# Sampled memory attention in eight units instead of twelve, the spread of token factors one place later

## The chip, the cores and the metric

The kernel runs on one core of one Trainium2 chip. The metric is the device time of one execution in microseconds (us); the median of three runs of the kernel before is 2639.46 us (2638.61 to 2641.45). The engines are TensorE (PE), VectorE (DVE), ScalarE (ACT) and GpSimd (POOL); SyncE (SP) issues most of the DMAs.

## The reference, cut to what matters

One inference step of a two-layer decoder trunk, for a prompt of 1024 tokens and for 8 samples of 8 tokens that share all weights. In every layer a mixing block is followed by cross-attention into a memory and by a convolutional feed-forward block. The change lies in the cross-attention, for the samples' part above all: each of the 8 samples has its own cached keys and values of 256 memory tokens, 4 heads of 128.

```python
def mem_attend(h, k, v, w_q, q_gain, w_o):
    q = rmsnorm((h @ w_q).reshape(N, T, MEM_HEADS, MEM_HD), q_gain)
    s = jnp.einsum('nthd,nmhd->nhtm', q, k) * (MEM_HD ** -0.5)
    pr = jax.nn.softmax(s, axis=-1)
    o = jnp.einsum('nhtm,nmhd->nthd', pr, v)
    return o.reshape(N, T, MEM_WIDTH) @ w_o
...
    xp = xp + mem_attend(rmsnorm(xp, ln_mem[l]), mk, mv, m_w_q[l], m_q_gain[l], m_w_o[l])
    xs = xs + mem_attend(rmsnorm(xs, ln_mem[l]), cache_mem_k[l], cache_mem_v[l], m_w_q[l],
                         m_q_gain[l], m_w_o[l])
    fp, cp = conv_ffn(rmsnorm(xp, ln_ffn[l]), zc, f_w_up[l], ...)
```

## The kernel before

The 1088 tokens lie in nine tiles of 128 (the last, tile 8, has the 64 sample tokens) and in three chunks of 384, 384 and 320 columns. `mem(l, rs)` does the cross-attention of one layer and runs twice, once per layer; `ffn(l)` follows each time.

`mem` first loops over the nine tiles: `qproj` (the query projection, matmuls at L259 to L261), `scores` of the tile before (L830), its softmax on DVE and ACT, and `trp` of the tile before that, which transposes the probabilities (L167 from `k`, copies at L846 and L847). Then comes the out-projection: for each chunk c two halves of four blocks m, and for each (c, m) one product of twelve matmuls (L259 to L261) that writes a `psa` buffer. `x_out` adds the old x to it (DVE L323, L325), squares it (ACT L303) and adds the square to the chunk's sum `acc` (L305, on DVE for odd m, on POOL for even m), and stores the new x by SP in `xq` (L330).

The samples' attention is cut into pieces by the generator `all_samples()`, and the program calls `next(parts)` between the products. Two sets a and b hold four samples each. Their pieces are:
- `keys(j)`: load sample j's keys (512 KB, SP, one of three stage buffers `st`), 16 transposes in two groups (L167 from `st`) into two PSUM buffers, copied by DVE (L884) and ACT (L882) to a `k` tile
- `score`: 32 matmuls (L890); `softmax` (L810 to L822, and four loads of values by SP)
- `trans`: two transposes and a copy (L906); `values`: 16 matmuls (L912), then DVE L915 and L918; `finish`: one transpose and a copy (L924)

Behind the products of a chunk stand `norm_chunk(c)`, which sums `acc` over the partitions (PE L352, then DVE L335 and three powers on POOL, L336), and `factors(c)`, that is `spread`: three diagonals on DVE (L387), three matmuls that spread them over the partitions (PE L388) and a copy into `rvq` (DVE L391). `build()` multiplies x by `rvq` (DVE L1094, `hx`) and makes the operands of `ffn`'s first products from it (L1105, L1106, L1111); their weights come by L1061 and are split at L1069 and L1070.

The order of PE is the order in which the program is written; the other engines' orders are set by a scheduler at build time. `psA()` and `psB()` hand out PSUM buffers `psa` and `psb`, four of each. Loads and stores go through SP's queue in order.

Before, the samples' pieces stand so. `a.keys(0)` follows tile 7 in the loop and `a.keys(1)` stands ahead of the out-projection; both use `psa`. With chunk 0's products m = 3, 4, 5 come `a.keys(2)`, `a.keys(3)`, the score of a; with chunk 1's products m = 1, 4, 5, 6 the trans of a, its values, `b.keys(0)`, `b.keys(1)`; with m = 7 the finish of a and `b.keys(2)`. At j == 4, between chunk 1 and chunk 2, stand `b.keys(3)`, the score of b, `norm_chunk(1)`, `factors(1)`, `build()` and the rest of b. `norm_chunk(0)` and `factors(0)` follow chunk 1's product m = 2.

Of the kernel before, what the change touches and what calls it, by code (L numbers as in the profile page):

```python
# [71 lines left out]
def kernel(  # L72
# [22 lines left out]
    def f(ap):  # L95
        return ap.bitcast(F32)
# [4 lines left out]
    def psB():  # L101
        return pb.tile([128, 512], F32, tag="b", name="psb")
# [48 lines left out]
    def small(tag="s", w=8, bufs=12):  # L151
        return sm.tile([128, w], F32, tag=tag, name=tag, bufs=bufs)
# [117 lines left out]
    def tile_of(t):  # L270
        return t // 3, (t % 3) * 128, (128 if t < 8 else 64)
# [76 lines left out]
    def norm_chunk(c):  # L348
        ps = psB()
        for t in range(3 * c, 3 * c + 3):  # L350
            _, o, w = tile_of(t)
            mm(ps[:w, 2 * (t % 3):2 * (t % 3) + 2], lhsT=acc[c][:, o:o + w], rhs=ones[:, 0:2], start=True, stop=True)  # L352
        for t in range(3 * c, 3 * c + 3):
            w = tile_of(t)[2]
            xr[t] = small(f"r{t}", 1, 1)
            rsq(xr[t][:w], ps[:w, 2 * (t % 3):2 * (t % 3) + 1], 1.0 / D)
# [384 lines left out]
    def mem(l, rs):  # L741
# [4 lines left out]
        def factors(c, pl=tmp):  # L746
            o, n = CHS[c]
            spread(c, xr, pl, rvq[:, o:o + n])

        with ExitStack() as es:  # L750
# [17 lines left out]
            def build():  # L768

                tcp = es.enter_context(pool(f"mem{l}tc"))  # L770
                R["tc"] = 1
                for j in range(4):
                    up_operands(l, 0, j, xq, rvq, B0, tcp)
# [153 lines left out]
            def all_samples():  # L927
                a, b = Samples(0), Samples(1)
                for x, y in ((a, None), (b, a)):
                    x.keys(0, psB if y else psA)  # L930
                    yield
                    x.keys(1, psB if y else psA)
                    yield
                    if y:
                        y.finish()
                    x.keys(2)
                    yield
                    x.keys(3)
                    yield
                    x.score()  # L940
                    x.softmax()
                    for _ in range(4):
                        yield
                    x.trans()
                    for _ in range(3):
                        yield
                    x.values()
                    yield
                yield
                yield  # L950
                b.finish()

            for i in range(NT):
# [7 lines left out]
                if i == 6:  # L961
                    parts = all_samples()
# [4 lines left out]
            for j, (hf, c) in enumerate([(0, 0), (1, 0), (0, 1), (1, 1), (0, 2), (1, 2)]):  # L967
                o, n = CHS[c]
                if j == 4:
                    for _ in range(2):  # L970
                        next(parts)
                    norm_chunk(1)
                    factors(1)
                    build()
                    for _ in parts:
                        pass
                if hf == 0 and c:
                    sp = [split_act(s3p, n, otf[:, k, o:o + n]) for k in range(4)]
                    if c == 2:
                        old = []  # L980
                        for i in range(4):
                            rd = f(s3p.tile([128, 2, 384], F32R, tag="s3", name="rd"))[:, :, :n]
                            nc.sync.dma_start(out=rd, in_=xd[:, 2 * i:2 * i + 2, :])
                            old += [rd[:, 0], rd[:, 1]]
                for m in range(4 * hf, 4 * hf + 4):
                    ps = psA()
                    w = wo[m // 2]
                    mo = 128 * (m % 2)
                    for k in range(4):
                        mm3(ps[:, :n], w[:, 0, k, mo:mo + 128], w[:, 1, k, mo:mo + 128], sp[k][:, 0, :n], sp[k][:, 1, :n], k == 0, k == 3)  # L990
                    x_out(c, m, ps, xq, [old[m]] if c == 2 else [f(xh[c][:, m, :]), f(xl[c][:, m, :])], rvq[:, o:o + n] if c == 2 else None)
                    if c == 0 and m == 1:
                        trp(7)
                    elif c == 0 and m == 2:
                        trq(8)
                        expand_q()
                        pv(2)
                        es2.close()
                        rvp = rs.enter_context(tc.tile_pool(name=f"rv{l}", bufs=1, reuse_waits="tile", side="right"))
                        rvq = rvp.tile([128, 1088], F32, name="rvq")  # L1000
                        gtail = rvp.tile([128, 18, HB], F32, name="gtail")
                    elif c > 0 or m > 2:
                        next(parts, None)
                    if c == 1 and m == 2:
                        norm_chunk(0)
                        factors(0)
        return xq, rvq, gtail, B0, factors

# [805 lines left out]
```

## Time and profile before

| | |
|---|---|
| median of three runs | 2639.46 us (2638.61 to 2641.45) |
| the profiled execution | 2642.09 us |
| its span, first to last instruction | 2640.3 us |
| mean granted TensorE clock | 0.965 of full speed |
| PE busy | 2494.3 us, 94% of the span |
| DVE busy | 1971.8 us, 75% |
| ACT busy | 1235.5 us, 47% |
| POOL busy | 447.6 us, 17% |

The profile is that of one execution, and its own time stands beside its span: durations below come from it. A busy share is a mean over all stages. The first `mem` lies at some 337 to 556 us of the span, the second at some 1690 to 1900. Rows give a start in us, a duration in us, the engine, the line of the kernel and the tile, the number of instructions in the row (x8), and in brackets the idle time of the engine just ahead and what ended it. In rows of matmuls the ends overlap with the next start.

### The profile page before, as it was taken

Reading aid. Unit: us, or ns where it says so; the run is one execution under the profiler, and the core shown is the slowest. Engines: PE = TensorE matmul, PEld = TensorE weight load, DVE = VectorE, ACT = ScalarE, POOL = GpSimd, SP = SyncE. Lnnn points to the kernel's source line nnn. Section 1 sums busy time; section 2 is a strip of 40 time slices with the busy share of each in tenths; the row PEclk is TensorE's granted clock in tenths of the full one; section 3 lists DMA queues with packets and bytes.
Section 4 is the critical chain, followed back from the end, with each engine's and each line's share of the span. In section 5 each row is a group of like instructions: output and inputs, shape, how many; then the busy total and the mean of one; then the engine's idle time right before and its main releaser. Section 6 shows DMA issues by size and latency. Waiting matters only on the chain. (4 is left out here: it accounts for less than half of the span.)

```text
span 2640.3 us, 46213 instructions
## 1 busy us (share of the span) xinstructions
PE 2494.3 (94%) x17136; PEld 2311.1 (88%) x17136; DVE 1971.8 (75%) x4551; ACT 1235.5 (47%) x2705; POOL 447.6 (17%) x418
## 2 busy tenths in 40 slices
PE   8999999779999998999999989998699999989898
PEld 7998988679999998999876768887599999989898
DVE  7646965797878786788767777856987878776885
ACT  7324645355554544333555554552555554544231
POOL 2516532110000001110133333421100000011100
PEclk9999999889999999999999998999799999999999
DMA  8302213533334236654211021115333334256642
GB/s 276 117 12 71 64 37 104 169 96 121 125 99 133 95 126 216 209 192 140 67 39 48 1 65 58 59 41 179 105 106 127 121 111 133 92 182 249 218 144 83
DMA packets 229345, 305.53 MB, mean 116 GB/s; under 512 B 17793, under 2 KB 189919, under 8 KB 229118
## 3 DMA queue, kind: packets, MB, share of 16 engines
q1 hardware_dynamic: 215806, 236.82, 28.3%
q0 software_dynamic: 13312, 65.74, 6.8%
q8 instruction: 135, 2.21, 0.4%
q14 instruction: 92, 0.75, 0.1%
HBM read 217.79 MB, written 84.63 MB: 115 GB/s over the span
## 5 line engine op out<-in xcount | busy, mean ns | idle before, releaser
L1069 ACT ACTIVATE w<-st 128x512 fp32r<-128x512 f32 (+2 forms) x532 | 299.9, 572 | 396.9 <-PE psb L1023 116.2
L1070 DVE TENSOR_TENSOR w<-st,w 128x512 fp32r<-128x512 f32 (+2 forms) x532 | 325.9, 617 | 175.0 <-ACT w L1069 167.5
L1021 PE MATMUL psa<-b,w 128*128 128x272 f32 x1056 | 309.2, 293 | 41.2 <-ACT b L1105 12.2
L1022 PE MATMUL psa<-b,w 128*128 128x272 f32 x1056 | 307.1, 291 | 10.1 <-DVE b L1106 10.1
L1021 PE MATMUL psa<-big,w 128*128 128x272 f32 x1056 | 309.8, 293 | 3.7 <-ACT x L1379 1.7
L1023 PE MATMUL psa<-big,w 128*128 128x272 f32 x1056 | 309.3, 293 | 0.5 <-DVE w L1070 0.5
L1022 PE MATMUL psa<-big,w 128*128 128x272 f32 x1056 | 308.3, 292 | 0.0
L1023 PE MATMUL psa<-b,w 128*128 128x272 f32 x1056 | 307.7, 291 | 0.0
L1021 PEld LDWEIGHTS psa<-b,w 128*128 128x128 f32 x1056 | 201.0, 190 | 44.8 <-ACT b L1105 12.8
L1021 PE MATMUL psb<-b,w 128*128 128x272 f32 x792 | 230.6, 291 | 0.0
L1023 PE MATMUL psb<-b,w 128*128 128x272 f32 x792 | 230.3, 291 | 0.0
L1023 PE MATMUL psb<-big,w 128*128 128x272 f32 x792 | 229.4, 290 | 0.5 <-DVE w L1070 0.5
L1021 PE MATMUL psb<-big,w 128*128 128x272 f32 x792 | 229.0, 289 | 0.0
L1022 PE MATMUL psb<-b,w 128*128 128x272 f32 x792 | 229.0, 289 | 0.0
L1022 PE MATMUL psb<-big,w 128*128 128x272 f32 x792 | 228.3, 288 | 0.0
L260 PE MATMUL psa<-s,w 128*128 128x384 f32 (+1 forms) x576 | 198.6, 345 | 15.3 <-DVE s L361 15.0
L1022 PEld LDWEIGHTS psa<-b,w 128*128 128x128 f32 x1056 | 201.2, 191 | 12.5 <-DVE b L1106 12.5
L1021 PEld LDWEIGHTS psa<-big,w 128*128 128x128 f32 x1056 | 202.5, 192 | 6.1 <-ACT x L1379 2.2
L1023 PEld LDWEIGHTS psa<-big,w 128*128 128x128 f32 x1056 | 203.5, 193 | 0.7 <-DVE w L1070 0.7
L1022 PEld LDWEIGHTS psa<-big,w 128*128 128x128 f32 x1056 | 202.8, 192 | 0.0
L259 PE MATMUL psa<-s,w 128*128 128x384 f32 (+1 forms) x576 | 199.0, 345 | 3.1 <-ACT s L360 3.1
L1023 PEld LDWEIGHTS psa<-b,w 128*128 128x128 f32 x1056 | 201.1, 190 | 0.0
(365 smaller groups left out, 6584.2 us busy)
## 6 DMA issues: line engine op xcount, KB each, us to landing
st<-in_f_w_up_dram SPq DMA_DIRECT2D x88, 512.0 KB
hd<-big SPq DMA_DIRECT2D x264, 136.0 KB
hd<-m SPq DMA_DIRECT2D x176, 136.0 KB
big<-hd POOLq DMA_DIRECT2D x48, 408.0 KB, 6.5
st<-in_f_w_down_dram SPq DMA_DIRECT2D x48, 384.0 KB
b<-hd POOLq DMA_DIRECT2D x18, 816.0 KB, 7.0
big<-hd POOLq DMA_DIRECT2D x18, 816.0 KB, 7.1
ks<-in_m_w_kv_dram SPq DMA_DIRECT2D x16, 512.0 KB
```

What stands on the lines that cost most here:

```text
L259: mm(out, lhsT=ah, rhs=bh, start=first, stop=False)
L260: mm(out, lhsT=ah, rhs=bl, start=False, stop=False)
L1021: mm(ps[:, :QT], lhsT=wt[:, 0, k, :], rhs=bt[:, 0, k, :], start=first and k == 0, stop=False, skip_group_check=True)
L1022: mm(ps[:, :QT], lhsT=wt[:, 0, k, :], rhs=bt[:, 1, k, :], start=False, stop=False, skip_group_check=True)
L1023: mm(ps[:, :QT], lhsT=wt[:, 1, k, :], rhs=bt[:, 0, k, :], start=False, stop=k == nk_of(j) - 1, skip_group_check=True)
L1069: S.activation(t[:, 0], src, AF.Copy)
L1070: V.tensor_tensor(out=t[:, 1], in0=src, in1=f(t[:, 0]), op=ALU.subtract)
```

## The change

The keys pieces of a set are joined in pairs, so a set has eight calls instead of twelve, and the free calls behind a score and a trans become fewer (four yields to three, three to two). At j == 4 the norm of chunk 1 stands first, then one piece, then the second spread. The first spread is called two products after its norm instead of directly behind it.

```diff
                 for x, y in ((a, None), (b, a)):
                     x.keys(0, psB if y else psA)
-                    yield
                     x.keys(1, psB if y else psA)
                     yield
                     if y:
                         y.finish()
                     x.keys(2)
-                    yield
                     x.keys(3)
                     yield
                     x.score()
                     x.softmax()
-                    for _ in range(4):
+                    for _ in range(3):
                         yield
                     x.trans()
-                    for _ in range(3):
+                    for _ in range(2):
                         yield
                     x.values()
                     yield
@@
                 if j == 4:
-                    for _ in range(2):
-                        next(parts)
                     norm_chunk(1)
+                    next(parts)
                     factors(1)
                     build()
                     for _ in parts:
@@
                     if c == 1 and m == 2:
                         norm_chunk(0)
+                    elif c == 1 and m == 4:
                         factors(0)
```

The calls fall so afterwards: `a.keys(0)` and `(1)` behind tile 7 (in `psa`), `a.keys(2)` and `(3)` ahead of the out-projection (in `psb`); in chunk 0 the score of a with m = 3 and its trans with m = 6; in chunk 1 its values with m = 0, `b.keys(0)` and `(1)` with m = 1, the finish of a and `b.keys(2)` and `(3)` with m = 2, followed by `norm_chunk(0)`; the score of b with m = 3, `factors(0)` behind m = 4, the trans of b with m = 6, nothing with m = 7. At j == 4 come `norm_chunk(1)`, the values of b, `factors(1)`, `build()` and the finish of b.

PE ahead of the out-projection, the place at which the first product of chunk 0 starts; L830 is scores(7), `k_4008` are the probabilities of tile 6, `st` a stage buffer with a sample's keys:

```order
 L830 MATMUL psb<-kt,qt 128x256 x4
 L167 MATMUL psb<-idt,k_4008 128x128 x8
-L167 MATMUL psa<-idt,st 128x128 x8
+L167 MATMUL psb<-idt,st 128x128 x16
 L259 MATMUL psa<-s_3942,w 128x384
 L260 MATMUL psa<-s_3942,w 128x384
```

Eight transposes of keys into two `psa` buffers have become sixteen into four `psb` buffers, right behind the two `psb` buffers of scores(7) and the two of `trp`. Likewise behind tile 7 eight transposes into `psa` have become sixteen.

DVE around the first spread, before (norm 0 at L335, the diagonals at L387, `rvq` at L391):

```order
L323 TENSOR_TENSOR t<-psa,big 128x384
L335 TENSOR_SCALAR s<-psb 128x1 x3
L325 TENSOR_TENSOR t<-t,big 128x384
L387 TENSOR_SCALAR t<-idt,r_4547 128x128
L387 TENSOR_SCALAR t<-idt,r_4551 128x128
L387 TENSOR_SCALAR t<-idt,r_4555 128x128
L391 COPY rvq<-psb 128x384
```

And DVE at the same spread in the changed program (here L810 to L822 are the softmax of b and L1074 is a sum of `ffn`'s weights, which waits for their load; the changed file has two lines less above them):

```order
L325 TENSOR_TENSOR t<-t,big 128x384
L1074 TENSOR_TENSOR st<-st 128x4x128
L810 TENSOR_REDUCE s<-psb 128x1
L305 TENSOR_TENSOR acc_4497<-acc_4497,t 128x384
L813 TENSOR_SCALAR s<-s 128x1
L821 RECIPROCAL s<-s 128x1
L822 TENSOR_TENSOR t_4681<-t_4681,s 128x256
L323 TENSOR_TENSOR t<-psa,big 128x384
L325 TENSOR_TENSOR t<-t,big 128x384
L387 TENSOR_SCALAR t<-idt,r_4623 128x128
L387 TENSOR_SCALAR t<-idt,r_4627 128x128
L387 TENSOR_SCALAR t<-idt,r_4631 128x128
```

The diagonals, which stood next to the norm, now stand behind b's softmax and the next x update.

PE at the end of chunk 1, before (`k_4723` and `k_4738` are the last two key tiles of b, `k_4768` to `k_4774` its values):

```order
L890 MATMUL psb<-k_4723,qm 32x256
L890 MATMUL psb<-k_4738,qm 32x256
L352 MATMUL psb<-ones,acc_4492 128x2 x3
L388 MATMUL psb<-t,ones 128x128 x3
L167 MATMUL psb<-idt,t_4776 128x128 x2
L912 MATMUL psb<-k_4768,t_4915 32x512
L912 MATMUL psb<-k_4770,t_4915 32x512
```

And in the changed program, from the last matmul of chunk 1's last product on (`k_4673` to `k_4679` are b's values):

```order
L261 MATMUL psa<-s_4478,w 128x384
L352 MATMUL psb<-ones,acc_4497 128x2 x3
L912 MATMUL psb<-k_4673,t_4768 32x512
L912 MATMUL psb<-k_4675,t_4768 32x512
L912 MATMUL psb<-k_4677,t_4768 32x512
L912 MATMUL psb<-k_4679,t_4768 32x512
L912 MATMUL psb<-k_4673,t_4768 32x512
L912 MATMUL psb<-k_4675,t_4768 32x512
L912 MATMUL psb<-k_4677,t_4768 32x512
L912 MATMUL psb<-k_4679,t_4768 32x512
L388 MATMUL psb<-t,ones 128x128 x3
L167 MATMUL psb<-idt,t_4818 128x128
```

The norm now follows the product, and the values of b stand between the norm and the spread instead of behind it.

## Rows read from the trace of the kernel before

**Rows 1.** The list of PE's waits between 380 and 560 us, the first `mem`: tile and line that waited, what ended the wait, us in total, how often, the longest.

```profile
PE psa L1021 <- ACT b L1105: 6.1, 1, 6.1
...
PE psb L167 <- DVE k L822: 0.6, 1, 0.6
```

**Rows 2.** PE's timeline behind the last product of chunk 1.

```profile
485.96 0.27 PE L167 MATMUL psb<-idt,t 128*128 128x128 f32 x1
486.07 1.91 PE L167 MATMUL psb<-idt,st 128*128 128x128 f32 x16
...
491.41 3.25 PE L890 MATMUL psb<-k,qm 128*32 128x256 f32 x26 [2.87 <-ACT k L882]
494.58 0.83 PE L352 MATMUL psb<-ones,acc 128*128 128x2 f32 x6
498.02 1.74 PE L388 MATMUL psb<-t,ones 128*128 128x128 f32 x6 [2.61 <-DVE t L387]
...
500.74 4.78 PE L912 MATMUL psb<-k,t 128*32 128x512 f32 x16 [0.55 <-DVE t L906]
```

**Rows 3.** DVE's timeline from the second `rvq` copy on.

```profile
499.80 0.56 DVE L391 COPY rvq<-psb 128x384 f32<-128x384 f32 x1 [0.89 <-PE psb L388]
500.27 0.41 DVE L906 COPY t<-psb 128x256 f32<-128x256 f32 x1
500.60 2.86 DVE L1094 SCALAR_TENSOR_TENSOR hx<-big,vec,rvq 128x544 f32<-128x544 f32 x4
...
506.55 0.68 DVE L915 TENSOR_TENSOR t<-psb,cst 128x512 f32<-128x512 f32 x1
...
537.79 0.28 DVE L335 TENSOR_SCALAR s<-psb 128x1 f32<-128x1 f32 x3 [1.02 <-PE psb L352]
539.07 0.74 DVE L1070 TENSOR_TENSOR w<-st,w 128x512 fp32r<-128x512 f32 x1 [1.00 <-ACT w L1069]
```

**Rows 4.** Stretches of the span: length, then busy us (and instructions) of PE, PE's weight loads, DVE, ACT and POOL, the granted clock, the DMA engines' busy share and GB/s.

```profile
247.00:251.00 4.00, 3.62 (x16) 3.56 (x17) 1.86 (x3) 1.87 (x4) 2.95 (x4) 0.67 0.16 37
470.00:473.50 3.50, 3.50 (x13) 3.50 (x14) 0.56 (x1) 0.00 (x0) 0.00 (x0) 0.53 0.49 136
510.00:532.00 22.00, 20.71 (x120) 19.83 (x120) 21.96 (x52) 12.89 (x32) 4.60 (x6) 0.82 0.27 86
```

**Rows 5.** The same moments in the second `mem`: PE at the end of chunk 1's last product and at the values of b, and DVE's second `rvq` copy.

```profile
1831.38 0.27 PE L167 MATMUL psb<-idt,t 128*128 128x128 f32 x1
1845.81 4.02 PE L912 MATMUL psb<-k,t 128*32 128x512 f32 x16 [0.55 <-DVE t L906]
...
1844.87 0.56 DVE L391 COPY rvq<-psb 128x384 f32<-128x384 f32 x1 [0.89 <-PE psb L388]
```

**Rows 6.** Pieces of the samples' attention between products, on PE: the score and the values of a; and DVE's L305 at the end of the x update whose product ended at 453.09.

```profile
453.09 1.94 PE L890 MATMUL psb<-k,qm 128*32 128x256 f32 x32
475.99 1.93 PE L912 MATMUL psb<-k,t 128*32 128x512 f32 x16
...
455.07 0.56 DVE L305 TENSOR_TENSOR acc<-acc,t 128x384 f32<-128x384 f32 x1 [0.72 <-ACT t L303]
```

**Rows 7.** PE's timeline at the keys of a: behind tile 7, and ahead of the out-projection.

```profile
417.14 1.04 PE L167 MATMUL psa<-idt,st 128*128 128x128 f32 x8
417.93 0.47 PE L259 MATMUL psa<-w,big 128*64 128x512 f32 x1
...
431.26 1.04 PE L167 MATMUL psb<-idt,k 128*128 128x128 f32 x8
432.13 1.04 PE L167 MATMUL psa<-idt,st 128*128 128x128 f32 x8
432.92 0.42 PE L259 MATMUL psa<-s,w 128*128 128x384 f32 x1
```

**Rows 8.** DVE's timeline (four rows) and ACT's (one row) at these places: the readers of the PSUM buffers.

```profile
419.14 0.69 DVE L630 TENSOR_TENSOR t<-psa,s 128x512 f32<-128x512 f32 x1
419.75 0.68 DVE L884 COPY k<-psa 128x512 f32<-128x512 f32 x1
...
433.10 0.74 DVE L847 COPY s<-psb 128x256 f32<-128x256 f32 x2
...
434.61 0.67 DVE L884 COPY k<-psa 128x512 f32<-128x512 f32 x1
...
434.54 0.47 ACT L818 ACTIVATE k<-psb,s 128x256 f32<-128x256 f32 x1
```

**Rows 9.** Two weight loads of `ffn`: SP's issues, and ACT's first instructions that waited for them.

```profile
486.11 0.39 SPq L1061 DMA_DIRECT2D st<-in_f_w_up_dram  x1
...
487.61 1.13 SPq L1061 DMA_DIRECT2D st<-in_f_w_up_dram  x2
...
490.24 0.63 ACT L1069 ACTIVATE w<-st 128x512 fp32r<-128x512 f32 x1 [2.50 <-DMA st<-in_f_w_up_dram]
...
492.69 0.63 ACT L1069 ACTIVATE w<-st 128x512 fp32r<-128x512 f32 x1 [0.92 <-DMA st<-in_f_w_up_dram]
```

**Rows 10.** PE's timeline at the first spread, which follows its norm.

```profile
468.16 0.90 PE L388 MATMUL psb<-t,ones 128*128 128x128 f32 x4 [1.70 <-DVE t L387]
469.84 0.49 PE L388 MATMUL psb<-t,ones 128*128 128x128 f32 x2 [0.77 <-DVE t L387]
```

**Rows 11.** PE's timeline in the first mixing block, a single wait.

```profile
247.38 1.10 PE L559 MATMUL psb<-bd,vt 64*128 64x64 f32 x8 [1.26 <-POOL vt L547]
```

## The prediction

> **What bounds the kernel now.** The profiled execution took 2642.09 us, its span 2640.3, so 1.8 us lie outside the span and are left alone. TensorE (PE) is busy 94% of the span, so whatever delays PE, or the engine that PE ends up waiting for, counts in full. I read the list of PE's waits around the first `mem` first: the long ones stand at its end [rows 1]. Then PE's timeline there: the last product of chunk 1 ends at 485.96, call that moment P. From P to 499.80 PE does key transposes, a score, a norm and the second spread, with two waits of 2.87 and 2.61 us in it [rows 2]. At 499.80 VectorE (DVE) copies the second factors into `rvq` and at once starts on the `hx` products of `build()`; call that moment R [rows 3]. From R on DVE has hardly a gap: 21.96 us of 22 busy in 510 to 532, and its idle pieces after R are 1.02 and 1.00 us [rows 3, 4]. PE, meanwhile, waits 6.1 us at the end of this stretch for operands made there [rows 1]. So the end of `mem` moves with R, not with the moment at which PE gets through its own list, and chunk 2's products have slack. The question is what the change does to R. R − P is 13.84 us in the first `mem` and 1844.87 − 1831.38 = 13.49 in the second [rows 2, 3, 5].
>
> **What goes.** Behind P the change leaves only `norm_chunk(1)`, `values` of b and the second spread ahead of R. The finish of a, sixteen transposes, the wait for ScalarE's key copy, the score (at half its normal rate) and the trans leave that place [rows 2]. That shortens P to R. The work does not vanish: it is done earlier, ahead of P.
>
> **What comes ahead of P, in work.** Sixteen key transposes 1.91 (486.07 row) and the finish 0.11 (485.96 to 486.07) [rows 2], one score 1.94 [rows 6], and the two transposes of trans, at 1.91 / 16 = 0.12 each, 0.24: 4.2 us. All of it is PE work in a stretch where PE was the engine that set the pace.
>
> **Waits ahead of P** come at four places.
>
> First, at i = 7 the two keys units of a now run together in `psA`, which has four buffers. Tile 7's projection still holds one, so the last of the four groups of four transposes finds none free and waits until DVE's L630 has read that projection, 419.14 + 0.69 = 419.83, while three groups would be through at 417.14 + 3 x 0.4 = 418.35. Tile 8's projection then waits for the first key copy, 419.75 + 0.68 = 420.43 [rows 7, 8]. The idle time is 1.5 + 0.2 = 1.65 (1.3 to 1.9).
>
> Second, ahead of the loop units 2 and 3 use `psB` straight behind scores(7) and trp(6), which hold all four buffers. Trp starts at 431.26 and ends at 432.13. The first group needs DVE's L847 (433.10, two in 0.74), the third ScalarE's second exponential (434.54 + 0.47 = 435.01), the fourth the copy of the first (about 434.6 + 0.68). The first product would then start at 435.7 instead of 432.92, that is 2.8 later, of which 0.8 is the eight additional transposes and 2.0 wait (1.6 to 2.3) [rows 7, 8]. Against this the wait of 0.59 for the softmax of tile 7 at L167 goes, since its result is ready by then [rows 1].
>
> Third, unit 3 of b needs the stage buffer of unit 0, which is now given back only one product, one finish and two units earlier, some 4 us. No view shows a key load's landing; the nearest rows are two weight loads of the same 512 KB: 486.11 to 490.24 and 487.61 to 492.69, 4.1 and 5.1 us until the instruction that waited ran [rows 9]. A wait between nothing and some 1.4 (5.1 less 4, and an issue); I take 0.8, towards the middle.
>
> Fourth, the first spread. Before, it ran right behind its norm and cost 1.70 + 0.77 = 2.47 us of waiting, in which GpSimd's three powers were made [rows 10]. Two products later the powers are long done, so at first sight this 2.47 is won. But DVE executes in order, and in the new order (second excerpt above) the diagonals L387 stand behind the sum of weights L1074, the whole softmax of b and the x update of the product just finished, L323 and L325. Two adds of 0.56 and the diagonals of 0.29 each behind the product's end give at least 1.5; a late weight load or exponential makes it 3.0. I take 2.47, no gain.
>
> Sum ahead of P: 4.2 + 1.65 + 2.0 + 0.8 − 0.59 + 0 = +8.1. The bounds are 4.2 + 1.3 + 1.6 + 0 − 0.59 − 1.0 = 5.5 and 4.2 + 1.9 + 2.3 + 1.4 − 0.59 + 0.5 = 9.7.
>
> **The clock.** Behind the 2.47 us of waiting at 468 the granted clock was 0.53 over 470 to 473.5, the lower of the two levels (1.2 against 2.4 GHz) [rows 4, 10]. PE was busy throughout, so 3.5 x 0.47 = 1.6 us are lost. A single wait of 1.26 at 247.38 was followed by the same thing, 0.67 over 247 to 251 [rows 4, 11]. The spell behind the spread is in both kernels. The two new waits, ahead of tile 8 and ahead of the loop, are of the same size as these, so each may cost another 1.6. The first is nearly one piece of 1.5 and I count it whole; the second is in pieces with transposes between them, and I count half: 2.4 (0 to 3.2). That makes P later by 10.5.
>
> The Trainium skill, "TensorE: Matmul & The Clock Gate", section "A second HAM failure mode: psum-queue depth-cycling", says that short PE pauses between groups of matmuls that cycle through PSUM banks can make the clock swing, and that throughput suffers from the swing and not from the single matmul. By that rule both new bank waits would be followed by a slow spell (3.2); if it did not apply here the sum would lose its 2.4 and the case be that of no change below. No run here shows it for these banks yet; the rows at 247 and 470 show waits for data, not for banks.
>
> **From P to R afterwards.** The norm now follows the product directly, so it waits for L323, L325, L303 and L305 of block 7: product end to end of L305 was 453.09 to 455.63, 2.54 [rows 6]. Before, the key transposes and the score covered this. Then the norm 0.83 [rows 2], `values` 1.93 at full rate [rows 6] or 4.02 as in the second `mem` [rows 5] (the 4.78 of the first is near it), I take 3.0 because it follows a wait; under it GpSimd's powers and the diagonals are hidden. Then the spread 1.74 and the copy [rows 2]. Together 8.2 (6.8 to 10.0) instead of 13.84: 5.6 won.
>
> **Behind R.** The copy L906 and the product L915 of b's tail (0.41 and 0.68, or 0.33 and 0.60 to the next start) now lie ahead of R [rows 3]: 0.93 less in the full stretch. The finish and the split of chunk 2 come earlier against R, which only lengthens PE's wait of 6.1. Two idle pieces of 1.02 and 1.00 may shrink or be replaced by others of that size; I leave them.
>
> **The sum.** Per `mem` +10.5 − 5.6 − 0.9 = +4.0; twice, +8.0: the profiled 2642.09 becomes 2650.1. The median of the runs, 2639.46, is 2.6 below that execution, so the forecast is 2647.5.
>
> **The rivals.** The two sides of the sum are of one size, so rivals are near.
>
> *No slow spells.* The new waits are there but the clock stays up, and `values` runs at 2.2: P +8.1, P to R −6.4, tail −0.9, so +0.8 per `mem`, +1.6 in all: 2641.1. For it speaks that the waits are broken up by transposes; against it the 1.26 us wait that did drop the clock.
>
> *Faster.* The bank waits ahead of the loop do not bite: the buffers come free in time because DVE and ScalarE, relieved of copies at those places, run ahead. Then 3.65 goes and no spell comes with it: P +4.45, less 6.4 and 0.9: −2.85 per `mem`, 2633.8. It decides the sign as soon as P is later by less than 7.3, and a clear gain (over 0.2%, 5.3 us, about what a measurement of this kernel can tell from no change) needs under 4.7. Against it: the times of L630, L847 and L818 are DVE's and ScalarE's own chains behind the projection and the scores, and the change moves none of them forward.
>
> *More is lost.* All bounds on the bad side, +9.7 and 3.2 of clock, `values` at 4.0 or more with R − P at 10.0 (3.8 won), no gain in the tail: +9.1 per `mem`, 2657.7. A late load for b's unit 3, or a weight split ahead of the diagonals that waits for its load, would do it.
>
> **Numbers.** My forecast with its neighbours, slower by over 0.2%, 0.47; more lost, 0.13; no slow spells 0.27; faster 0.13. The range reaches from between the faster and the unchanged case to the larger loss: 2637.5 to 2657. Faster by over 0.2% 0.13, within 0.2% 0.27, slower 0.60.
>
> **What would show it.** In the changed profile: at L167 `psa` and `psb` from `st` waits for DVE L630, L847 and ScalarE L818 totalling 3 to 4 us, and the granted clock near 0.5 behind them; P near 496; L352 waiting 2.5 for L305; no wait of L890 for a key copy; the second `rvq` copy near 504.5 instead of 499.80, and the wait of L1021 near 6 or longer. If that copy comes before 499, the front waits were overrated; if it comes at 504 but the whole is no longer, R does not set the end.

## The result and the profile after

The changed kernel is slower: 2653.48 us median of eight runs (2645.77 to 2660.19) against 2639.03 of eight runs of the kernel before (2630.91 to 2647.46), a ratio of 1.0062 with a 95% interval of 1.0042 to 1.0081, that is 16.4 us (11 to 21). The forecast was 2647.5, slower, with a range to 2657.

The profiled execution of the changed kernel took 2645.77 us (span 2644.0), the fastest of its eight; beside the 2642.09 of before it shows only 3.7 us. So the two spans as such mislead, and the stretches must be read. Take each `mem` from PE's first L341 in it to the end of its last long wait, the one of 6 us for operands of `ffn`. Rows of PE's timeline before:

```profile
346.23 0.28 PE L341 MATMUL psb<-ones,acc 128*128 128x2 f32 x2
...
556.22 0.59 PE L1021 MATMUL psa<-b,w 128*128 128x272 f32 x1 [6.11 <-ACT b L1105]
...
1695.75 0.28 PE L341 MATMUL psb<-ones,acc 128*128 128x2 f32 x2
...
1901.42 0.59 PE L1021 MATMUL psa<-b,w 128*128 128x272 f32 x1 [6.10 <-ACT b L1105]
```

And after (two lines less in the file, so L1019 for L1021):

```profile
345.84 0.28 PE L341 MATMUL psb<-ones,acc 128*128 128x2 f32 x2
...
563.20 0.60 PE L1019 MATMUL psa<-b,w 128*128 128x272 f32 x1 [6.41 <-ACT b L1103]
...
1699.40 0.28 PE L341 MATMUL psb<-ones,acc 128*128 128x2 f32 x2
...
1913.78 0.59 PE L1019 MATMUL psa<-b,w 128*128 128x272 f32 x1 [6.33 <-ACT b L1103]
```

The first pass takes 217.4 instead of 210.0 us. The second begins at 1695.75 before and 1699.40 after, so it takes 214.4 instead of 205.7. Together 16.1 us, the measured loss. What hid it in the spans are the stretches outside the passes: 3.3 us less between them, and from 1901.42 to PE's last matmul group at 2630.92 before, 729.5 us, from 1913.78 to 2635.44 after, 721.7. A wait for `x` accounts for 4.6 of it: the sum of L1021 (L1019 after) for it behind 1914 was 7.2 us before and 2.6 after. In the other kernels below this last stretch varies as much (719 to 729), whatever was changed in `mem`, so I count it as chance of one execution; no run was made to show that.

PE's waits of the changed kernel between 380 and 570 us, as in [rows 1]:

```profile
PE psa L1019 <- ACT b L1103: 6.4, 1, 6.4
...
PE psb L388 <- DVE t L387: 3.9, 1, 3.9
...
PE psb L352 <- DVE acc L305: 2.7, 1, 2.7
...
PE psa L167 <- DVE t L630: 1.4, 1, 1.4
PE psb L167 <- DVE s L847: 1.3, 1, 1.3
PE psb L167 <- DMA st<-in_cache_mem_k_dram: 0.5, 1, 0.5
PE psb L167 <- ACT k L818: 0.5, 1, 0.5
```

All the forecast new waits are there. PE's timeline at the places of [rows 2, 7, 10]:

```profile
419.49 1.47 PE L167 MATMUL psa<-idt,st 128*128 128x128 f32 x12
422.34 0.63 PE L167 MATMUL psa<-idt,st 128*128 128x128 f32 x4 [1.37 <-DVE t L630]
...
488.53 1.62 PE L388 MATMUL psb<-t,ones 128*128 128x128 f32 x6 [3.93 <-DVE t L387]
...
501.18 1.44 PE L352 MATMUL psb<-ones,acc 128*128 128x2 f32 x6 [2.69 <-DVE acc L305]
502.55 3.64 PE L912 MATMUL psb<-k,t 128*32 128x512 f32 x16
```

P, the end of chunk 1's last product, is 501.18 − 2.69 = 498.5. From the first keys of a to P 79.0 us instead of 68.8 [rows 2, 7]: +10.2, and +10.5 in the second pass. From DVE's timeline, as [rows 3]:

```profile
507.80 0.56 DVE L391 COPY rvq<-psb 128x384 f32<-128x384 f32 x1 [0.85 <-PE psb L388]
...
509.20 2.86 DVE L1092 SCALAR_TENSOR_TENSOR hx<-big,vec,rvq 128x544 f32<-128x544 f32 x4
```

From P to R 9.3 instead of 13.84; from R to the end 55.4 instead of 56.4 (second pass 57.4 instead of 56.6). These three stretches give +4.6 and +7.4. The rest of the 7.4 and 8.7, 2.7 and 1.3 us, lies ahead of a's first keys, where I had looked for nothing: PE's first wait in the pass, for DVE's L630 of tile 0, is longer. Here the wait and the stretch behind it (columns as in [rows 4]), before:

```profile
353.88 0.81 PE L167 MATMUL psb<-idt,t 128*128 128x128 f32 x4 [3.14 <-DVE t L630]
...
353.88:359.10 5.22, 5.22 (x21) 4.47 (x21) 0.23 (x2) 1.37 (x2) 0.54 (x1) 0.67 0.01 3
```

And after:

```profile
354.99 1.09 PE L167 MATMUL psb<-idt,t 128*128 128x128 f32 x4 [4.66 <-DVE t L630]
...
354.99:361.80 6.81, 6.81 (x21) 5.74 (x22) 1.49 (x4) 1.37 (x2) 0.95 (x2) 0.57 0.10 36
```

The wait is 1.5 us longer, and at the lower clock the stretch behind it loses 6.81 x 0.43 = 2.9 instead of 5.22 x 0.33 = 1.7 us: 2.7 together. SP's issue of weights before:

```profile
325.63 0.38 SPq L240 DMA_DIRECT2D st<-in_m_w_o_dram  x1
```

And what precedes the wait after, in the timelines of SP, ACT and POOL:

```profile
325.25 0.38 SPq L874 DMA_DIRECT2D st<-in_cache_mem_k_dram  x1
...
345.24 0.38 SPq L240 DMA_DIRECT2D st<-in_m_w_o_dram  x1
...
349.25 1.06 ACT L233 ACTIVATE w<-st 128x1024 fp32r<-128x1024 f32 x1 [1.64 <-DMA st<-in_m_w_o_dram]
...
350.39 2.34 POOL L234 TENSOR_TENSOR w<-st,w 128x1024 fp32r<-128x1024 f32 x1 [1.32 <-ACT w L233]
```

Before, the issue at 325.63 was the load of the out-projection's first weights. Now a's unit 1, which comes ahead of those weights in the program, takes that stage buffer, and the weights follow at 345.24. ACT waits for them ahead of tile 0's L623, and POOL's split stands ahead of tile 0's power: L630 comes 1.5 us later in this pass, 1.3 in the second (a wait of 2.10 instead of 0.79, with the granted clock at 1.00 behind it).

### The profile page after: what moved, and what is told of

Same layout as the page of the kernel before. It is cut to its first block, busy times and chain, and to the rows that moved or that the text cites. A ratio compares the mean times of both kernels' runs of the same rounds, so it can differ in the third digit from the quotient of the medians.

```text
span 2644.0 us, 46227 instructions
## 1 busy us (share of the span) xinstructions
PE 2492.4 (94%) x17136; PEld 2311.5 (87%) x17136; DVE 1970.3 (75%) x4551; ACT 1235.6 (47%) x2705; POOL 447.6 (17%) x418
## 4 chain that ended last, share of the span: by engine, by line
PE 56%; issue 20%; DVE 14%; DMA 6%; ACT 2%; POOL 2%; SPq 0%; POOLq 0%; ACTq 0%; DVEq 0%
PE psa L259 6%; PE psa L260 6%; PE psa L1019 6%; PE psa L261 6%; PE psa L1020 6%; PE psa L1021 6%; PE psb L1020 4%; PE psb L1021 4%; PE psb L1019 4%; DVE s L361 3%; PE psb L167 2%; DMA st<-in_f_w_down_dram 1%; PE psb L855 1%; DMA big<-hd 1%; DVE w L1068 1%
## 5 line engine op out<-in xcount | busy, mean ns | idle before, releaser
L1019 PE MATMUL psa<-b,w 128*128 128x272 f32 x1056 | 309.1, 293 | 36.6 <-ACT b L1103 12.7
L1019 PE MATMUL psa<-big,w 128*128 128x272 f32 x1056 | 309.7, 293 | 13.1 <-ACT big L1103 9.6
L1021 PE MATMUL psa<-big,w 128*128 128x272 f32 x1056 | 308.8, 292 | 0.0
L1021 PE MATMUL psa<-b,w 128*128 128x272 f32 x1056 | 307.9, 292 | 0.0
L1019 PEld LDWEIGHTS psa<-b,w 128*128 128x128 f32 x1056 | 200.8, 190 | 40.1 <-ACT b L1103 13.3
L1019 PE MATMUL psb<-big,w 128*128 128x272 f32 x792 | 230.3, 291 | 3.9 <-ACT big L1103 3.9
L1021 PE MATMUL psb<-big,w 128*128 128x272 f32 x792 | 230.2, 291 | 0.0
L1021 PE MATMUL psb<-b,w 128*128 128x272 f32 x792 | 229.3, 290 | 0.0
L1019 PE MATMUL psb<-b,w 128*128 128x272 f32 x792 | 229.3, 290 | 0.0
L1019 PEld LDWEIGHTS psa<-big,w 128*128 128x128 f32 x1056 | 202.5, 192 | 15.6 <-ACT big L1103 10.1
L1021 PEld LDWEIGHTS psa<-big,w 128*128 128x128 f32 x1056 | 203.1, 192 | 0.0
L1021 PEld LDWEIGHTS psa<-b,w 128*128 128x128 f32 x1056 | 200.8, 190 | 0.0
```

The lines of the kernel that those rows point to most:

```text
L1019: mm(ps[:, :QT], lhsT=wt[:, 0, k, :], rhs=bt[:, 0, k, :], start=first and k == 0, stop=False, skip_group_check=True)
L1021: mm(ps[:, :QT], lhsT=wt[:, 1, k, :], rhs=bt[:, 0, k, :], start=False, stop=k == nk_of(j) - 1, skip_group_check=True)
```

## The experiments

The ratio is to the kernel before; "passes" is the sum of both `mem` passes in the one profiled execution, as measured above; a difference of ratios is turned into us by 2638.

| kernel | ratio (95% interval) | passes, us |
|---|---|---|
| before | 1 | 415.7 |
| changed | 1.0062 (1.0042 to 1.0081) | 431.7 |
| e1 a apart | 1.0015 (1.0001 to 1.0029) | 425.3 |
| e2 first spread back | 1.0029 (1.0018 to 1.0040) | 425.9 |
| e3 values first | 1.0058 (1.0042 to 1.0074) | 429.5 |
| e4 weights first | 1.0028 (1.0012 to 1.0045) | 428.2 |
| e5 e1, e2 and e3 together | 1.0007 (0.9994 to 1.0020) | 417.7 |
| e7 e1 and e2 together | 1.0033 (1.0020 to 1.0047) | 419.5 |
| e8 mixed | 1.0012 (1.0000 to 1.0025) | 416.7 |
| e10 spread behind b's score | 1.0002 (0.9990 to 1.0015) | 417.7 |
| e11 before, a joined | 1.0052 (1.0034 to 1.0071) | 428.7 |
| e12 e11, weights first | 1.0047 (1.0032 to 1.0061) | 423.7 |
| e6 before, spread late | 0.9980 (0.9965 to 0.9994) | 408.3 |
| e9 e6, norm ahead of score | 0.9991 (0.9972 to 1.0010) | 414.4 |

**Where does the loss sit? e1 to e4 undo one thing each in the changed kernel.**

e1, a's units apart (`if not y: yield` behind unit 0 and unit 2, and one free call less behind score and trans):

```diff
                     x.keys(0, psB if y else psA)
+                    if not y:
+                        yield
                     x.keys(1, psB if y else psA)
@@
                     x.keys(2)
+                    if not y:
+                        yield
                     x.keys(3)
@@
-                    for _ in range(3):
+                    for _ in range(3 if y else 2):
@@
-                    for _ in range(2):
+                    for _ in range(2 if y else 1):
```

> The changed kernel with set a's keys units apart again (unit 0 behind tile 7, unit 1 ahead of the out-projection, units 2 and 3 with chunk 0's products m = 3 and 4, the score with m = 5), the free calls behind them fewer, so that everything from a's values on stands as in the changed kernel. Theory A (the loss is the sum of the stretches of the two `mem` passes): the waits of L167 for DVE L630, L847 and ScalarE L818 go (1.4 + 1.3 + 0.5 per pass, 0.6 for L822 comes back), and the first wait for L630 in the pass falls from 4.7 to 3.1 in the first and from 2.1 to 0.8 in the second, because the first out-projection weights are loaded ahead of unit 1 again; about 4 us per pass, so 8 us less than the changed kernel, 6 us above the kernel before. Theory B (the early waits are absorbed later, because the end of a pass hangs on loads and on VectorE): no more than 2 us less than the changed kernel, so still 12 or more above the kernel before.

2641.58 us median, 3.7 above the kernel before by the medians and 12.4 (6 to 19) below the changed kernel by the ratios: theory A, above its 8 us. The passes say 6.5 less. The wait at 354 is back at 3.16, those at the keys of a are gone; the first spread waits longer instead, 4.31 and 5.40 us.

e2, the first spread back:

```diff
                         norm_chunk(0)
-                    elif c == 1 and m == 4:
                         factors(0)
```

> The changed kernel with the first spread back directly behind its norm (chunk 1, m = 2), all else as changed. Theory A: VectorE's diagonals stand ahead of the weight piece that waits for its load, PE's wait for L387 falls from 3.9 to about 2.5, and the slow spell behind it from 6.0 to 3.5 us in length: 2.5 us per pass, 5 us less than the changed kernel, some 9 above the kernel before. Theory B: the late weight load holds VectorE all the same and PE waits for the next thing that VectorE owes it, so less than 1.5 us changes in all.

1.0029 instead of 1.0062: 8.7 us (3 to 15) by the ratios, 5.9 by the passes, theory A. PE's timeline shows the wait at its old size:

```profile
477.71 0.68 PE L388 MATMUL psb<-t,ones 128*128 128x128 f32 x4 [1.97 <-DVE t L387]
478.88 0.49 PE L388 MATMUL psb<-t,ones 128*128 128x128 f32 x2 [0.48 <-DVE t L387]
```

e3, values ahead of the norm (`next(parts)` one line up, ahead of `norm_chunk(1)`):

> The changed kernel with the values of b ahead of the second norm at the end of chunk 1, instead of behind it, all else as changed. Theory A: the values (1.9 us at full rate) now run while the last block's sum is made, PE's wait of L352 for L305 falls from 2.7 to below 1, but GpSimd's powers and the diagonals are no longer covered by the values, about 2.4 us from the norm to the first spread; from the last product's end to the second `rvq` copy 6.6 instead of 9.4 us, so 2.8 per pass and 5 to 6 us less than the changed kernel. Theory B: the moment of that copy does not set the end of the pass, or the values' loads are not there yet and PE waits for them: no change, or a wait of L912 for a load.

The mechanism came, the time did not. PE and DVE:

```profile
495.76 1.92 PE L912 MATMUL psb<-k,t 128*32 128x512 f32 x16
498.44 0.80 PE L352 MATMUL psb<-ones,acc 128*128 128x2 f32 x6 [0.76 <-DVE acc L305]
501.11 1.74 PE L388 MATMUL psb<-t,ones 128*128 128x128 f32 x6 [1.87 <-DVE t L387]
...
502.89 0.56 DVE L391 COPY rvq<-psb 128x384 f32<-128x384 f32 x1 [0.89 <-PE psb L388]
```

From P (495.76) to R 7.1 us in both passes, 2.2 to 2.4 less than in the changed kernel. The ratio is 1.0058, and 5 us less lie at the edge of what the two intervals allow. By itself this run leaves it open; e5 against e7, the same edit in a kernel without the other losses, is 1.0007 against 1.0033, some 7 us (2 to 12). The passes give the edit 2.3 us here and 1.8 there.

e4, the out-projection's first load ahead of a's joined units:

```diff
                 if i == 7:
+                    wo = [load_cols(m_w_o[l], 0, k=4)]
                     next(parts)
@@
-            wo = [load_cols(m_w_o[l], 256 * i, k=4) for i in range(4)]
+            wo += [load_cols(m_w_o[l], 256 * i, k=4) for i in range(1, 4)]
```

> The changed kernel with the first load of the out-projection's weights placed ahead of a's keys units 0 and 1 in the program, so that it takes the early stage buffer and unit 1 a later one, all else as changed. Theory A: ScalarE no longer waits for that load ahead of tile 0's L623 and GpSimd's split of it no longer stands ahead of tile 0's powers, so PE's first wait for L630 falls from 4.7 to 3.1 in the first pass and from 2.1 to 0.8 in the second; 1.3 to 1.5 per pass, about 3 us less than the changed kernel. Theory B: the 1.5 us are given back at the next wait of the projection loop or unit 1's later load makes PE wait behind tile 7: no change or a new wait of L167 for a load.

The first wait for L630 is 3.17 and 0.79 again, as theory A has it. The time fell by 9 us (2 to 16) by the ratios, 3.5 by the passes; the wait is worth 3.

**The front part alone: e11 and e12** join a's units in the kernel before, with two free calls added behind them for set a so that the rest keeps its place; e12 has e4's edit as well.

> The kernel before with set a's keys units joined in pairs as in the changed kernel (units 0 and 1 behind tile 7, units 2 and 3 ahead of the out-projection), two free calls behind them so that all else stays at its place. Theory A: per pass 1.4 us for the first weight load of the out-projection that gives up its early stage buffer, 1.4 + 1.3 + 0.5 − 0.6 = 2.6 for buffers, and nothing of it is absorbed before the end of the pass: 4 us per pass, 8 above the kernel before. Theory B (the loss of the changed kernel comes from its later places alone and the early waits are absorbed): within 2 us of the kernel before.

> The kernel before with set a's keys units joined as in the changed kernel and the out-projection's first weight load placed ahead of them. Its distance to the kernel with the joined units alone is the price of the stage buffer; its distance to the kernel before is that of the PSUM buffers. Theory A (prices as PE's waits show them): the first wait for L630 is back at 3.1 and 0.8 us, the waits behind tile 7 and ahead of the out-projection stay at 1.4, 1.3 and 0.5, so 5 to 6 us above the kernel before and 3 below the joined units alone, or more below them if the late load costs at other places too. Theory B (the load order does not matter for the time): equal to the joined units alone, 12 or more above the kernel before.

e11 is 13.7 us (9 to 19) above the kernel before: joining a's units costs nearly as much alone as the whole change, and nothing of it is absorbed. PE's waits are those of the changed kernel:

```profile
418.39 0.63 PE L167 MATMUL psa<-idt,st 128*128 128x128 f32 x4 [1.37 <-DVE t L630]
...
434.50 1.09 PE L167 MATMUL psb<-idt,st 128*128 128x128 f32 x8 [1.27 <-DVE s L847]
436.09 1.09 PE L167 MATMUL psb<-idt,st 128*128 128x128 f32 x8 [0.50 <-ACT k L818]
```

These (less the 0.6 for L822, which goes) and its longer first waits for L630 (4.50 and 3.31 instead of 3.14 and 0.79) add up to 9 us in both passes. The passes are 13.0 longer: 3.7 ahead of a's first keys, 6.3 from there to P, 3.0 behind P, nearly all of these in the second pass. That last part has no wait of PE's that I could name. e12 took the longer L630 wait away (3.15 and 0.78), but its time fell by 1.3 us only, with intervals of 4 us on each side; its passes fell by 5.0. e4 and e12 answer differently by the ratios, 9 and 1, around the 3 that the wait is worth: that the wait comes and goes with the order of the loads is shown in every profile, what it is worth in time stays open.

**The late spread: e6, e10.** e6 is the kernel before with `factors(0)` moved behind m = 4, as in the changed kernel, and nothing else.

> The kernel before with one part of the change alone, the first spread behind chunk 1's product m = 4, where a's values stand in this kernel. Theory A (what made the spread late in the changed kernel was the piece of weights that VectorE had to wait for, and that no piece of PE's stood between the product and the spread): here no weight piece stands ahead of the diagonals and a's values (1.9 us) cover the x update, so PE's wait for L387 falls from 2.47 us to below 0.5 and the slow spell behind it goes, 3 to 4 us per pass, 6 to 8 less than the kernel before. Theory B (a late spread costs as such, because the diagonals queue behind x updates): the wait stays at 2 us or more and the time does not change.

0.9980 (0.9965 to 0.9994), 5 us faster than the kernel before and the fastest of all: theory A, a little under its 6 to 8; the passes are 7.4 shorter. PE's timeline, and its granted clock (the figure ahead of the last two) over this stretch:

```profile
464.46 0.72 PE L352 MATMUL psb<-ones,acc 128*128 128x2 f32 x6
...
469.39 1.93 PE L912 MATMUL psb<-k,t 128*32 128x512 f32 x16
471.51 0.91 PE L388 MATMUL psb<-t,ones 128*128 128x128 f32 x6 [0.20 <-DVE t L387]
```

```profile
464.00:480.50 16.50, 16.30 (x110) 14.47 (x109) 11.20 (x25) 4.12 (x8) 4.57 (x6) 1.00 0.53 143
```

The wait of 2.47 and the slow spell of [rows 4, 10] are both gone, and P comes 4.4 and 4.2 us sooner behind a's first keys, about what the two were worth (2.47 + 1.6). So the same move that makes PE wait longer in the changed kernel gains here. Two things differ: a's values stand between the product and the spread, and no piece of `ffn`'s weights stands ahead of the diagonals. e10 tells them apart. It is e5 with the spread behind b's score (`c == 1 and m == 3`).

> The kernel with set a apart and b's values ahead of the second norm, with the first spread behind b's score (chunk 1, m = 3): a piece of 1.9 us stands between the product and the spread, but two pieces of weights that wait for their loads still stand ahead of the diagonals on VectorE. Theory A1 (the weight loads are what made the spread of the changed kernel late): PE still waits 1.5 to 3 us for L387 and the slow spell follows; the time is that of the kernel with three parts undone or up to 4 us above it. Theory A2 (the missing cover was the cause): the wait falls below 0.5 us, the slow spell goes, and the time is 4 to 7 us below that kernel, that is 3 to 6 below the kernel before.

A1, with a longer wait than its 1.5 to 3: with 1.9 us of cover PE still waits 3.70 (4.78 in the second pass). PE, DVE and ACT in e10, where L1072 and L1071 are the weight pieces:

```profile
473.84 1.93 PE L890 MATMUL psb<-k,qm 128*32 128x256 f32 x32
...
479.47 0.91 PE L388 MATMUL psb<-t,ones 128*128 128x128 f32 x6 [3.70 <-DVE t L387]
...
477.36 0.69 DVE L1072 TENSOR_TENSOR w<-st,w 128x512 fp32r<-128x512 f32 x1 [2.86 <-ACT w L1071]
...
479.04 0.67 DVE L387 TENSOR_SCALAR t<-idt,r 128x128 f32<-128x128 f32 x3
...
476.70 0.63 ACT L1071 ACTIVATE w<-st 128x512 fp32r<-128x512 f32 x1 [2.71 <-DMA st<-in_f_w_up_dram]
```

A load holds ACT, ACT's piece holds DVE, and the diagonals queue behind it. The time shows no loss by it: 1.0002 against e5's 1.0007, and the same 417.7 for the passes, though from a's first keys to P e10 is 1.2 and 2.0 us longer than e5. The changed kernel has the same chain; the last row is SP's issue of the first of these loads:

```profile
482.52 0.63 ACT L1067 ACTIVATE w<-st 128x512 fp32r<-128x512 f32 x1 [2.43 <-DMA st<-in_f_w_up_dram]
...
483.19 0.69 DVE L1068 TENSOR_TENSOR w<-st,w 128x512 fp32r<-128x512 f32 x1 [2.16 <-ACT w L1067]
...
473.85 0.45 SPq L1059 DMA_DIRECT2D st<-in_f_w_up_dram  x1
```

b's keys, read earlier, free their stage buffers earlier, so that the first of these weight loads is issued at 473.85, 25 us ahead of P, instead of 486.11, at P [rows 2, 9], and the scheduler puts their pieces ahead of the diagonals. In the changed kernel b's softmax stands between the piece and the diagonals as well (third excerpt of the change), with a wait of 0.69 for ACT in it; e10 has none there and waits as long, so the load is enough, but the softmax's own share in the 3.93 was not separated.

**What the part behind P is worth: e5, e7, e8, e9.** e5 is the changed kernel with e1's, e2's and e3's edits, e7 with e1's and e2's.

> The changed kernel with set a's keys units apart, the first spread directly behind its norm, and b's values ahead of the second norm: of the change there stays the merging of b's keys units, that is b's sixteen transposes, score and trans moved ahead of chunk 1's last product. Theory A (stretches add up): the last product's end of chunk 1 comes 4.7 us later in each pass than in the kernel before (work moved ahead and a wait for b's unit 3), from it to the second `rvq` copy 7.2 instead of 13.84 us; 1.9 us less per pass, so 3 to 4 us less than the kernel before. Theory B (moving work between the two sides of that product gives nothing, since what is won behind it comes back as weight loads that are not there yet): equal to the kernel before within 2 us.

> The changed kernel with set a's keys units apart and the first spread directly behind its norm; b's values stay between the second norm and the spread. Theory A: from the last product's end to the second `rvq` copy 9.5 us, 2.3 longer than with the values first, so this is 4 to 5 us above that kernel and within 2 us of the kernel before. Theory B (that stretch does not set the end of the pass): equal to the kernel with the values first.

e5 equals the kernel before (1.0007), with P to R 7.8 and 7.4 us and P later by 6.0 and 7.9 behind a's first keys: moving b's work ahead of P gives nothing in all. That is the time of its theory B, but P came later than theory A's 4.7, and no late load of weights is shown to be why. e7 is 7 us slower than e5 by the ratios, more than A's 4 to 5 and in its direction; by the passes it is 1.8. Its P to R was 7.6 us in the first pass and 10.0 in the second, where 9.5 was expected: behind the norm's wait of 2.97 and 3.23 the granted clock was 1.00 in the one and 0.50 in the other.

e8 is e5 with a's units 2 and 3 joined behind m = 3 (so one free call more):

> As the kernel with three parts undone (set a apart, first spread back, b's values first), but a's units 2 and 3 joined with chunk 0's product m = 3 and the score one place earlier, so that a's values' loads have a product more time. Theory A: where the loads of values came late PE waits no more (0.4 us at L912 in one profiled execution), and nothing else changes: equal to that kernel within 2 us, or 1 less. Theory B: joining units costs bank waits wherever they are joined: a new wait of L167 for a copy of the unit before, 1 us or more per pass.

Equal to e5 within the intervals. The waits for the values' loads went, a wait of 0.7 for the key copy came.

e9 is e6 with the norm moved into the gap at j == 4:

```diff
                 if j == 4:
-                    for _ in range(2):
-                        next(parts)
+                    next(parts)
                     norm_chunk(1)
+                    next(parts)
                     factors(1)
```

> The kernel before with two edits: the first spread behind chunk 1's product m = 4 (behind a's values), and at the end of chunk 1 the second norm between b's last keys unit and b's score instead of behind the score, so that b's score runs while GpSimd makes the powers. Theory A (the moment of the second `rvq` copy sets the end of the pass): from the last product's end to that copy 10.5 us instead of 13.4, since the wait of 2.4 us of the spread for its diagonals goes; 2.5 to 3 us less per pass than the kernel with the late spread alone, 10 to 12 less than the kernel before. Theory B (what is won there comes back behind that copy as waits for weight loads): no more than 1.5 per pass, 6 to 8 less than the kernel before.

A miss: 0.9991, no better than e6. PE now waits for the block sums, and DVE shows why:

```profile
487.32 1.41 PE L352 MATMUL psb<-ones,acc 128*128 128x2 f32 x6 [4.38 <-DVE acc L305]
...
485.64 0.69 DVE L1071 TENSOR_TENSOR w<-st,w 128x512 fp32r<-128x512 f32 x1 [2.10 <-ACT w L1070]
...
486.61 0.56 DVE L305 TENSOR_TENSOR acc<-acc,t 128x384 f32<-128x384 f32 x1 [0.28 <-ACT t L303]
```

Again a weight piece that waits for its load stands ahead on DVE. P to R stays at 12.9 and 13.1, and from the first `hx` to the end it is 59 to 60 us instead of 56. Part of b's softmax now lies behind R, and DVE is idle there for 5.8 instead of e6's 2.3 us in the first pass, 2.3 of it for another weight piece.

**What the ratios and the passes agree on.** Some edits were made in two kernels and so have two answers. By the ratios, the first spread back is worth 8.7 us in the changed kernel (e2), but with a apart it costs 4.7 (e7 against e1), and a apart is worth 12.4 (e1), but with the spread back it costs 1 (e7 against e2). By the passes the two answers are alike: 5.9 and 5.8 for the spread, 6.5 and 6.4 for a apart, 2.3 and 1.8 for the values first. Undone one after the other (e1, e7, e5), these three take the passes from 431.7 over 425.3 and 419.5 to 417.7, 14.0 us less, and the ratios of the two ends say 14.5. So both show that these three parts make up nearly all of the loss. How it divides among them rests on one profiled execution of each kernel, and depends on the kernel: joined in the kernel before, a's units cost 13 us. For a single kernel the two measures differ by up to 6 us (e1 is 9.6 above the kernel before by the passes, 4.0 by the ratio); why stays open.

## Why the prediction was right, and where its sizes were off

**Direction and range were right**: 2653.5 lies within 2637.5 to 2657. The signs of both sides of the sum held: P later by 10.2 and 10.5 (10.5 forecast), P to R shorter by 4.5 and 4.0 (5.6 forecast). R to the end, forecast 0.9 shorter, was 1.0 shorter in the first pass and 0.9 longer in the second. The whole was +16 where +8.0 was forecast, twice as much. The sign "P near 496" came at 498.5 and the copy "near 504.5" at 507.8, for the reasons below.

**The work moved ahead, and the waits for buffers.** The mechanism was right here. Of the 1.65 behind tile 7, 1.37 came; of the 2.0 ahead of the loop, 1.27 + 0.50; of the 0.8 for unit 3's load, 0.52 and 0.49. Each a little smaller.

**The clock term failed.** I gave 2.4 us to slow spells behind the two waits for PSUM buffers, because two waits of that size in the kernel before had been followed by one [rows 4, 10, 11]. There were none; in the last line, the stretch behind the first spread:

```profile
419.49:422.84 3.35, 1.98 (x18) 1.66 (x16) 3.35 (x9) 1.80 (x7) 1.02 (x1) 1.00 0.29 94
422.84:438.45 15.61, 14.34 (x65) 9.14 (x63) 4.51 (x10) 8.69 (x17) 8.57 (x5) 1.00 0.49 149
438.45:441.00 2.55, 2.05 (x17) 1.81 (x18) 1.79 (x6) 2.03 (x9) 0.00 (x0) 1.00 0.04 10
...
488.53:494.50 5.97, 5.97 (x22) 5.97 (x23) 1.27 (x4) 0.28 (x1) 0.99 (x1) 0.54 0.87 325
```

The rule of the Trainium skill in "TensorE: Matmul & The Clock Gate", section "A second HAM failure mode: psum-queue depth-cycling", which I had set beside this, did not show at these waits; it speaks of pauses that come frequently, in each iteration, and I had applied it to single ones. That the total for P came out right is luck: some 2.5 us appeared elsewhere.

**They appeared at the first spread.** I took its wait unchanged at 2.47, with 3.0 as the bound; it was 3.93 and 4.18, and the slow stretch behind it 5.97 us at 0.54 instead of 3.5 at 0.53 [rows 4, 10]: 1.5 of waiting and 2.7 − 1.6 = 1.1 of clock. I had named the weight load as what would make it late, and put it in the bound instead of the sum. e6, with no weight piece ahead of the diagonals, waits 0.20; e10, with one and as much cover, waits 3.70.

**P to R was a bit longer than the 8.2 forecast**, 9.3 and 9.5: the norm took 1.44 instead of 0.83, at the lower clock behind its wait of 2.69, and the values 3.64 instead of 3.0.

**The term that was missing is the stage buffer at the start of the pass.** It made 2.7 and 1.3 us of the missing 8. I followed the loads of b and not those of a. The profile of before had the row (the load of weights issued at 325.63, twenty microseconds ahead of the next one), and the order of the loads on SP would have shown that unit 1 steps ahead of it.

**That R sets the end** held for the changed kernel (R to the end 55.4 and 57.4 against 56.4 and 56.6) and for e6, whose R and end moved together. e9 limits it: its copy came no more than 1.1 us sooner behind P than e6's, and from it to the end took 4.2 and 2.4 us longer.

**The rival of no slow spells** was right on the clock at the two buffer waits and wrong on the time: the spread and the start were not in it, and behind the norm's wait of 2.69 the clock was at the lower level, so that the values ran 3.64 and not its 2.2.

## What to carry to other kernels

Here, joining units of work that share a pool of buffers made PE wait for the slowest reader of that pool (not everywhere: the pair joined in e8 cost a wait of 0.7 and no time that shows); and a load that comes earlier in the program takes the buffer of another load far away, so after such a change follow every load that shares the pool, not only those that were moved. A step made later gains if work of its own engine covers it and no piece that waits for a load comes to stand ahead of what it needs; e6 shows the gain, e10 the wait that takes it away. And where an execution varies by more than the effect, compare the stretches that the change can touch, not two spans, and make an edit in two kernels before giving it a price.

## What the runs showed of the hardware

I had not expected that PE's single wait of 1.37 us for a PSUM buffer would leave the granted clock at 1.00, while one of 1.26 us in [rows 4, 11] was followed by 0.67. The other profiles show that the row of [rows 11] is no price. In all fourteen the same instruction waits 1.26 to 1.28 us at this place. In seven of them, the kernel before among them, the granted clock of the 4 us behind it is 0.62 to 0.76; in the other seven it is 1.00. The changed kernel is one of these, in the same stretch as [rows 4]:

```profile
247.00:251.00 4.00, 3.51 (x22) 3.44 (x23) 1.86 (x3) 1.88 (x4) 2.95 (x4) 1.00 0.16 37
```

The edits all lie behind it (the first `mem` begins at some 345 us). So the same wait behind the same work is followed by a slow spell in one execution and not in another. The waits for buffers at a's keys are more even: 4 us at 1.00 behind all 12 waits of 1.36 to 1.39 us for L630 in the six kernels with a's units joined, and behind 10 of the 12 of 1.26 to 1.28 us for L847. Nor does a longer wait decide it: behind waits of 2.10 us (changed kernel), 3.27 (e3) and 3.31 (e11) for L630 at the start of the second pass the clock was 1.00, behind 3.33 us (e2) it was 0.66. What decides was not tried. For a forecast it means that a slow spell behind a wait of 1 to 3 us enters with a chance, counted over several profiles, and not with the price of one row.
